# Filler matmuls dealt out 3-2-1 and 3-3-2 among three scans, and the opening's LoRA weights loaded ahead, in a two-layer diffusion trunk

## The chip, the cores and the metric

One core of one Trainium2 chip. The metric is device microseconds of one execution. Before the change three runs gave 3964.88, 3975.29 and 3981.9 us; their median, 3975.29 us, is the time before.

## What is computed

Two layers of one trunk over 256 context tokens (segment C) and 512 latent tokens (segment L), model width 1024, everything in float32. Each layer norms its input with shift and scale vectors that come from a conditioning vector (adaLN), projects it, and runs three mixers side by side: bidirectional RWKV-7 (8 heads of 64), bidirectional chunked gated DeltaNet (4 heads of 128) and grouped-query attention. The mixers' outputs are gated, merged and projected, then a SwiGLU follows. In the second layer the context is read but not written.

```
mod_x = (silu_c @ ada_w[l] + ada_b[l])[:, None, :]
sh1x, sc1x, g1x, sh2x, sc2x, g2x = jnp.split(mod_x, N_MOD, axis=-1)
hx = modulate(rmsnorm(x, norm1[l]), sh1x, sc1x)
px = jnp.split(hx @ lp['w_in'], IN_SPLIT_POINTS, axis=-1)
...
ya_x, _ = rwkv_branch(hx, px[0], lp, st_a)
yb_x, _ = gdn_branch(hx, px[1], px[2], lp, st_b)
yc_x = attn_latent(px[3], px[4], kc, vc, lp, cos, sin)
out_x = merge_branches(hx, ya_x, yb_x, yc_x, lp)
x = x + g1x * yx
x = x + g2x * swiglu(modulate(rmsnorm(x, norm2[l]), sh2x, sc2x), ffn_w1[l], ffn_w3[l], ffn_w2[l])
```

Both recurrences are computed in chunks of 64 tokens: inside a chunk with matmuls and the inverse of a small triangular matrix, from chunk to chunk with a state.

## The kernel before, in words

**Dense tiles.** A product of the whole input with 128 columns of a weight is a dense tile (`dense`, L251). Float32 accuracy comes from splitting each operand in a high and a low part, so each of the 8 blocks of the inner dimension takes three matmuls (`mm3`, L241 to L243): 24 matmuls of 512 columns for L (into `dL`) and 24 of 256 columns for C (into `dC`). The weight is loaded by SP into one of two buffers `wst` (L236), rounded by ACT to `whi` (L227), and the rest is formed by POOL as `wlo` (`split`, L231).

**Order.** Instructions are written in program order and a list scheduler puts them in order for each engine, by priority and by a simulated time; an engine then runs its instructions in that order. The priority is the place in the program, and `high_priority(offset)` moves a block ahead by so many instructions (HPG = 400 or 300 for DeltaNet, HPR = 700 for RWKV).

**The opening** (`build`, L280). The input segments `xC` and `xL` are loaded, squared (ACT, L386), summed (DVE, L388, `acc`), summed over partitions by a matmul (L390, `ssC`, `ssL`) and scaled. Four pieces of the adaLN vectors of layer 0 (`ada`, L338, pieces 0 to 3) are each 2 MB of weights in four loads (`adaw`, L345), 16 matmuls (`adaps`, L349, 8 in the program), an ACT copy (`adasb`, L351) and four small matmuls (`adamp`, L354); DVE adds the bias into `MOD` (L357). When all four are there, `norm1` writes the normed input in two parts, `hh` (ACT, L405) and `hl` (DVE or POOL, L407). Piece 0 is traced in the C turn of the loop, a first 96-column LoRA weight (`self.first`, `l1m`) in the L turn, pieces 1 to 3 after the loop.

**The first products** (`lora_g`, L757). They are the dense tile of `self.first`, then two of a 128-column LoRA weight (one with the shift mix, `l1m`, one without, `l1w`). In layer 0 that weight is loaded here; in layer 1 it was loaded in `norm1` and lies in `self.second`. From the first product come the DeltaNet decay rows (`brC`, `gcC`, `brL`, `gcL`), turned by small matmuls (`tsp`, L1205); from the last, the gate.

**The passes** (`layer`, L593). DeltaNet runs in 2 passes (p0, p1), RWKV in 4 (j0 to j3). A pass has three groups of four chunks, in the order C, L0, L1. A group has a preparation (for RWKV the matmuls `lps`, `aps`, `tps`, `tpv`; for DeltaNet `kkp`, `gtp`), the inverse of its eight triangular blocks (`inverse`, L878: DVE, ACT and POOL work with five rounds of 16 small matmuls `ips`, L931), and four steps, 0 to 3, each of which needs the state of the step before (RWKV: `Xp`, `Up`, `SP`, `Op`; DeltaNet: `KS`, `GU`, `GSO`). "L0 step 2" below is the stretch from the first `Xp` (or `KS`) of that step to the first of the next.

Between the groups the program places the pass's 8 units (dense tiles for the next pass or for the merge gates): after group number i it emits as many as a table says, DeltaNet by `GD`, RWKV by `RD`:

```
for grp, n in zip((("C", 0), ("L", 0), ("L", 1)), RD[j]):
    with tc.high_priority(offset=HPR[l]):
        self.r_group(j, *grp)
    self.fill(min(n, len(self.units) - keep))
self.flush(keep)
```

What is left is emitted after the three groups (`flush`), in DeltaNet and in RWKV's last pass with two units kept for the end.

Of the kernel before, what the change touches and what calls it, by code (L numbers as in the profile page):

```python
# [8 lines left out]
F32 = mybir.dt.float32  # L9
# [29 lines left out]
AD = (0, 1, 2, 3)  # L39
ORD = (1, 2, 3, 6, 5, 7, 4)  # L40
LOV = ((1,), (1, 3, 5))
GD = ((5, 4, 0), (5, 4, 0))
RD = ((4, 4, 0), (4, 4, 0), (4, 4, 0), (2, 2, 0))


PV = {}
# [157 lines left out]
class Prog:  # L204
# [75 lines left out]
    def build(self):  # L280
        nc, tc, A = self.nc, self.tc, self.A
        self.pend = {"L": [], "C": []}
        pool = lambda name, bufs=1, **k: tc.tile_pool(name=name, bufs=bufs, **k)
        with tc.block(name="whole", schedule_with_timeline_sim=True), pool("cst") as cst, pool("wp", 2) as wp, pool("pp", 2, space=bass.MemoryType.PSUM) as pp, \
                pool("dr", space=bass.MemoryType.DRAM) as dr, pool("hp") as hp, pool("sb", 2) as sb:
            self.cst, self.wp, self.pp, self.dr, self.hp, self.sb = cst, wp, pp, dr, hp, sb
            self.dC, self.dc = pp.tile([128, 2, TC], F32, name="dC", tag="dC", bufs=1), 0
            C = cst.tile([128, NCO], F32, name="C")
            nc.sync.dma_start(C, A["co"][:, 0:NCO])
            self.C = C  # L290
            self.scv = cst.tile([128, 8, 32], F32, name="scv")
            nc.sync.dma_start(self.scv, A["cv"])
            nc.scalar.activation(self.scv, self.scv, AF.Silu)
            self.xsrc = {"C": A["xT"][:, :, 0:TC], "L": A["xT"][:, :, TC:T]}
            self.vectors(0)
            with tc.tile_pool(name="nx", bufs=2, reuse_waits="tile") as nx:
                x = {}
                self.nb = 8
                self.segs = ["L", "C"]
                ss = self.sums()  # L300
                self.tables()
                for s, n in (("C", TC), ("L", TL)):
                    x[s] = nx.tile([128, KT, n], F32, name="x" + s, bufs=1)
                    nc.sync.dma_start(x[s], self.xsrc[s])
                    if s == "C":
                        self.ada(0, 0, nx, 8, bank=("dL", 2))
                    else:
                        self.first = self.split(self.lora(0, 384, 96, 2, nx)[:])
                    for k in range(KT):
                        self.squares(x[s][:, k, :], k, s, ss)  # L310
                    self.settle()
                    rs = sb.tile([128, TL + 4], F32, name="rs", tag="up", bufs=2)[:, :n]
                    self.rstd_from(rs, ss[s], 1.0 / D, self.co("cb", 0, 1))
                    for k in range(KT):
                        nc.vector.tensor_tensor(x[s][:, k, :], x[s][:, k, :], rs, ALU.mult)
                for i in range(1, 4):
                    self.ada(0, i, nx, 8, bank=("dL", 2))
                self.norm1(0, x, nx)
            for l in range(DEPTH):
                self.l, self.nb = l, SB[l]  # L320
                self.last = l == DEPTH - 1
                self.P, self.MOD = self.Ps[l], self.MODs[l]
                self.layer()
                if self.upto is not None and self.upto[0] == l:
                    break
# [9 lines left out]
        self.nc.sync.dma_start(self.Ps[l], self.A["pv"][l])  # L335
        self.MODs[l] = self.cst.tile([128, 48, 2], F32, name=f"MOD{l}")

    def ada(self, l, n, pool, bufs=4, share=False, tag="adaw", bank=("iv", 1)):  # L338

        nc, A = self.nc, self.A  # L340
        ps = self.pp.tile([128, 512], F32, name="adaps", tag=bank[0], bufs=bank[1])
        for q in range(4):
            w = (self.wp.tile([128, 2, 512], F32, name="adaw", tag="wst") if share and q % 2 else
                 pool.tile([128, 2, 512], F32, name="adaw", tag=tag, bufs=bufs))
            nc.sync.dma_start(w, A["ada"][l, n][:, 2 * q:2 * q + 2, :])  # L345
            for i in range(2):
                k = 2 * q + i
                g = k % 4
                nc.tensor.matmul(ps[32 * g:32 * g + 32, :], self.scv[:, k, :], w[:, i, :], start=(k < 4), stop=(k >= 4))  # L349
        sb = pool.tile([128, 512], F32, name="adasb", tag="adasb", bufs=1)  # L350
        nc.scalar.copy(sb, ps)  # L351
        mp = self.pp.tile([128, 4, 2], F32, name="adamp", tag=bank[0], bufs=bank[1])
        for m in range(4):
            nc.tensor.matmul(mp[:, m, :], sb[:, 128 * m:128 * m + 128], self.co("sel2"), start=True, stop=True)  # L354
        ob, _ = PV["ada_b"]
        b = self.Ps[l][:, ob + 4 * n:ob + 4 * n + 4].unsqueeze(2).to_broadcast([128, 4, 2])
        nc.vector.tensor_tensor(self.MODs[l][:, 4 * n:4 * n + 4, :], mp, b, ALU.add)  # L357
# [235 lines left out]
    def layer(self):  # L593
# [14 lines left out]
        with pool("sx") as self.sx:  # L608
# [10 lines left out]
            with pool("sg") as self.sc:  # L619
# [5 lines left out]
                for p in range(2):  # L625
# [5 lines left out]
                    self.g_begin(p)  # L631
                    for grp, n in zip((("C", 0), ("L", 0), ("L", 1)), GD[p]):
                        with tc.high_priority(offset=HPG[l]):
# [9 lines left out]
        with pool("sr") as self.sc:  # L643
# [17 lines left out]
            for j in range(4):  # L661
# [5 lines left out]
                keep = 2 if j == 3 else 0  # L667
                for grp, n in zip((("C", 0), ("L", 0), ("L", 1)), RD[j]):
                    with tc.high_priority(offset=HPR[l]):
# [87 lines left out]
    def lora_g(self):  # L757

        nc, A, l, sc = self.nc, self.A, self.l, self.sc
        self.GC, self.BR, self.rw, self.re, gh = {}, {}, {}, {}, {}  # L760
        if l:
            wq, wm = self.second
        else:
            wq, wm = self.lora(l, 256, 128, 2, sc)
            wm = self.split(wm[:])
        ps = self.dense(*self.first, self.h, self.S12)
        for s in self.S12:
            n = TL if s == "L" else TC
            self.gdn_rows(s, n, ps[s])
            if s not in self.segs:  # L770
                continue
            z = self.mixed(s, ps, self.shifted(ps[s], n, 1, 0.5, 32, 32), 32)
            nc.scalar.activation(z[0:32], z[0:32], AF.Tanh, scale=0.5)
            nc.vector.tensor_scalar(z[0:32], z[0:32], 0.5, 0.5, ALU.mult, ALU.add)

            g = sc.tile([128, n], F32R, name="ghx" + s, bufs=1)
            nc.scalar.copy(g[0:32], z[0:32])
            nc.vector.tensor_tensor(g[32:64], z[0:32], g[0:32].bitcast(F32), ALU.subtract)
            nc.scalar.copy(g[64:96], z[0:32])
            gh["x", s] = g  # L780
        psq, up = self.lora_dense(wq, wm, self.segs)
        for s in self.segs:
            n = TL if s == "L" else TC
            z = self.mixed(s, psq, up[s])
            nc.scalar.activation(z, z, AF.Tanh, scale=0.5)
            nc.vector.tensor_scalar(z, z, 0.5, 0.5, ALU.mult, ALU.add)
            g = sc.tile([128, n], F32R, name="ghg" + s, bufs=1)
            gl = sc.tile([128, n], F32R, name="glg" + s, bufs=1)
            nc.scalar.copy(g, z)
            nc.gpsimd.tensor_tensor(gl, z, g[:].bitcast(F32), ALU.subtract)  # L790
            gh["g", s] = (g, gl)
        for j in range(4):
            g2 = self.g2_weights(j)
            for s in self.segs:
                n = TL if s == "L" else TC
                ps = self.psd(s)
                self.mm3(ps, g2[0], g2[1], *gh["g", s], True, False)
                nc.tensor.matmul(ps, g2[2], gh["x", s][0:96], start=False, stop=True)
                z = self.zt("gj", n)
                nc.scalar.copy(z, ps)  # L800
                t0 = TC if s == "L" else 0
                nc.gpsimd.dma_start(self.gd[:, j, t0:t0 + n], z)
# [931 lines left out]
```

## Time and profile before

| | |
|---|---|
| median of 3 runs | 3975.29 us (3964.88 to 3981.9) |
| profiled execution, its own time | 3986.69 us |
| its span, first to last instruction | 3984.9 us |
| mean granted TensorE clock | 0.906 |
| busy: PE, PEld, DVE, ACT, POOL | 90%, 73%, 61%, 42%, 37% of the span |
| loaded and stored | 296.61 MB, mean 74 GB/s |

PE is the matmul stream of TensorE and PEld its weight loads, which run beside it. The granted clock is 1.0 or 0.5 at any moment, of 2.4 GHz; a mean between them says how much of a stretch was at half. The profiled execution was 11.4 us longer than the median.

In time, from the trace: the opening to 47 us, the LoRA products to 113 us, attention of layer 0 to 335 us, DeltaNet to about 812 us, RWKV to about 1480 us, merge and SwiGLU to 2220 us, then the same for layer 1: DeltaNet from about 2465, RWKV from about 2850 to 3460 us, and its tail to the end.

### The profile page before, as it was taken

What the parts mean: (1) busy time and instruction counts of PE and PEld (TensorE: products, weight loads), DVE (VectorE), ACT (ScalarE), POOL (GpSimd) and SP (SyncE); (2) the same over time, 40 slices, a digit from 0 to 9 for tenths busy, and PEclk for the clock granted to TensorE, in tenths of its full rate; (3) what the DMA queues carried; (4) which work ended last, traced back from release to release, by engine and by line L of the source; (5) the groups of instructions that cost most, each with busy time, mean ns of one, the idle gap of its engine ahead of it and who ended that gap; (6) DMA issues with size and microseconds to landing.
All of it is one profiled execution on the core that took longest, in us unless ns stands there. A gap on an engine that the chain in (4) does not pass through costs nothing. (4 is left out here: it accounts for less than half of the span.)

```text
span 3984.9 us, 69791 instructions
## 1 busy us (share of the span) xinstructions
PE 3572.3 (90%) x27704; PEld 2928.8 (73%) x27704; DVE 2426.7 (61%) x4776; ACT 1681.5 (42%) x3207; POOL 1465.1 (37%) x1738
## 2 busy tenths in 40 slices
PE   7987878999899989899999798889998999898998
PEld 4655667777777768789999656666777777677887
DVE  5386745326766746565555557965167786467776
ACT  5455534334444432333333646543343443234334
POOL 3223213244233315454444424414241333164554
PEclk7998878999799999999999899989796988699999
DMA  5501111111011126422222251102120111252232
GB/s 190 172 30 51 32 33 50 53 57 55 13 53 38 40 71 199 153 80 69 70 69 59 94 179 53 51 25 75 39 63 9 53 32 47 96 186 66 93 96 82
DMA packets 121174, 296.61 MB, mean 74 GB/s; under 512 B 15024, under 2 KB 41824, under 8 KB 120464
## 3 DMA queue, kind: packets, MB, share of 16 engines
q1 hardware_dynamic: 111408, 260.16, 20.9%
q0 software_dynamic: 9440, 31.99, 2.1%
q8 instruction: 218, 3.57, 0.4%
q14 instruction: 108, 0.88, 0.1%
HBM read 257.87 MB, written 34.23 MB: 73 GB/s over the span
## 5 line engine op out<-in xcount | busy, mean ns | idle before, releaser
L231 POOL TENSOR_TENSOR wlo<-wst,whi 128x512 fp32r<-128x512 f32 (+3 forms) x606 | 693.0, 1164 | 784.1 <-ACT whi L227 755.4
L227 ACT CAST whi<-wst 128x1024 fp32r<-128x1024 f32 (+3 forms) x303 | 266.0, 878 | 512.3 <-PE dC L243 193.4
L241 PE MATMUL dL<-hh,whi 128*128 128x512 f32 x1040 | 436.3, 420 | 21.3 <-ACT tg L710 4.5
L242 PE MATMUL dL<-hl,whi 128*128 128x512 f32 x1040 | 423.7, 407 | 3.7 <-DVE hl L407 2.3
L243 PE MATMUL dL<-hh,wlo 128*128 128x512 f32 x1040 | 422.8, 407 | 0.1
L241 PEld LDWEIGHTS dL<-hh,whi 128*128 128x128 f32 x1040 | 202.1, 194 | 79.6 <-issue 6.9
L242 PEld LDWEIGHTS dL<-hl,whi 128*128 128x128 f32 x1040 | 201.9, 194 | 51.5 <-issue 7.5
L241 PE MATMUL dC<-hh,whi 128*128 128x256 f32 x704 | 220.7, 313 | 18.4 <-ACT ct L371 9.3
L243 PEld LDWEIGHTS dL<-hh,wlo 128*128 128x128 f32 x1040 | 201.3, 194 | 48.3 <-issue 2.5
L242 PE MATMUL dC<-hl,whi 128*128 128x256 f32 x704 | 213.2, 303 | 4.8 <-DVE hl L407 2.4
L243 PE MATMUL dC<-hh,wlo 128*128 128x256 f32 x704 | 212.2, 301 | 0.0
L502 POOL TENSOR_TENSOR sl<-S,sh 128x512 fp32r<-128x512 f32 x110 | 152.7, 1392 | 154.8 <-ACT sh L501 115.4
L241 PE MATMUL q<-g2h,sh 128*128 128x384 f32 (+1 forms) x528 | 166.8, 318 | 16.3 <-DVE c L524 13.8
L241 PEld LDWEIGHTS dC<-hh,whi 128*128 128x128 f32 x704 | 144.9, 206 | 35.3 <-ACT ct L371 11.9
L242 PE MATMUL q<-g2l,sh 128*128 128x384 f32 (+1 forms) x528 | 166.6, 316 | 2.9 <-DVE g2l L447 2.9
L243 PE MATMUL q<-g2h,sl 128*128 128x384 f32 (+1 forms) x528 | 165.1, 314 | 0.0
L242 PEld LDWEIGHTS dC<-hl,whi 128*128 128x128 f32 x704 | 145.2, 206 | 13.0 <-issue 3.9
L501 ACT CAST sh<-S 128x512 fp32r<-128x512 f32 x176 | 105.0, 619 | 105.0 <-PE q L242 63.7
L243 PEld LDWEIGHTS dC<-hh,wlo 128*128 128x128 f32 x704 | 145.1, 206 | 3.2 <-issue 1.7
L524 DVE TENSOR_TENSOR c<-c,q 128x384 f32<-128x384 f32 (+1 forms) x220 | 106.0, 482 | 61.7 <-PE q L243 50.6
L241 PE MATMUL dL<-fh,whi 128*128 128x512 f32 x352 | 138.3, 393 | 3.0 <-ACT fh L578 1.6
L242 PE MATMUL dL<-fl,whi 128*128 128x512 f32 x352 | 138.1, 392 | 0.0
(545 smaller groups left out, 10008.8 us busy)
## 6 DMA issues: line engine op xcount, KB each, us to landing
adaw<-in_ada SPq DMA_DIRECT2D x96, 512.0 KB
wst<-in_win SPq DMA_DIRECT2D x68, 512.0 KB
wst<-in_wg SPq DMA_DIRECT2D x48, 512.0 KB
w<-in_f SPq DMA_DIRECT2D x45, 512.0 KB
wst<-in_f SPq DMA_DIRECT2D x43, 512.0 KB
t<-tg POOLq DMA_DIRECT2D x48, 256.0 KB, 2.6
tgL<-t SPq DMA_DIRECT2D x48, 256.0 KB
wst<-in_f SPq DMA_DIRECT2D x48, 256.0 KB
```

Of the source, the lines that this page charges most:

```text
L227: nc.scalar.copy(hi, wt)
L231: nc.gpsimd.tensor_tensor(lo[:, a:b], wt[:, a:b], hi[:, a:b].bitcast(F32), ALU.subtract)
L241: nc.tensor.matmul(ps, wh, xh, start=first, stop=False)
L242: nc.tensor.matmul(ps, wh, xl, start=False, stop=False)
L243: nc.tensor.matmul(ps, wl, xh, start=False, stop=last)
L501: nc.scalar.copy(hi, src)
L502: (nc.vector if i in LOV[l] else nc.gpsimd).tensor_tensor(lo, src, hi[:].bitcast(F32), ALU.subtract)
L524: add = lambda d, a, b: nc.vector.tensor_tensor(d, a, b, ALU.add)
```

## The change

1. The tables. In `layer`, after the groups C, L0 and L1 a pass emitted 5, 1 and 0 of its units (DeltaNet; the table's 4 met what was left) or 4, 4 and 0 (RWKV), and now emits 3, 2, 1 or 3, 3, 2; RWKV's last pass 2, 1, 1 in place of 2, 2, 0. In DeltaNet two units stay for the end, as before.
2. The opening. `ada` has 12 buffers for its weights in place of 8, and its small matmuls write to another bank of PSUM than the large ones. Pieces 1 to 3 are traced ahead of the L segment's squares, not after the loop.
3. The 128-column LoRA weight of layer 0 is loaded and its mixed part split in the opening, ahead of `norm1`; `lora_g` finds it in `self.second`.

```diff
-GD = ((5, 4, 0), (5, 4, 0))
-RD = ((4, 4, 0), (4, 4, 0), (4, 4, 0), (2, 2, 0))
+GD = ((3, 2, 1), (3, 2, 1))
+RD = ((3, 3, 2), (3, 3, 2), (3, 3, 2), (2, 1, 1))
...
                     if s == "C":
-                        self.ada(0, 0, nx, 8, bank=("dL", 2))
+                        self.ada(0, 0, nx, 12, bank=("dL", 2), mbank=("ch", 2))
                     else:
+
+                        for i in range(1, 4):
+                            self.ada(0, i, nx, 12, bank=("dL", 2), mbank=("ch", 2))
                         self.first = self.split(self.lora(0, 384, 96, 2, nx)[:])
...
-                for i in range(1, 4):
-                    self.ada(0, i, nx, 8, bank=("dL", 2))
+                wq, wm = self.lora(0, 256, 128, 2)
+                self.second = wq, self.split(wm[:])
                 self.norm1(0, x, nx)
...
-        mp = self.pp.tile([128, 4, 2], F32, name="adamp", tag=bank[0], bufs=bank[1])
+        mbank = mbank or bank
+        mp = self.pp.tile([128, 4, 2], F32, name="adamp", tag=mbank[0], bufs=mbank[1])
...
-        if l:
-            wq, wm = self.second
-        else:
-            wq, wm = self.lora(l, 256, 128, 2, sc)
-            wm = self.split(wm[:])
+        wq, wm = self.second
```

What the scheduler makes of it, at three places.

**The opening, on PE and SP.** PE before, from its first matmul to the first dense one:

```order
L349 MATMUL adaps<-adaw,scv 32x512 x4
L390 MATMUL ssC<-acc,C 128x256
L349 MATMUL adaps<-adaw,scv 32x512 x4
L354 MATMUL adamp<-C,adasb 128x2 x4
L349 MATMUL adaps<-adaw,scv 32x512 x6
L390 MATMUL ssL<-acc,C 128x512
L349 MATMUL adaps<-adaw,scv 32x512 x2
L354 MATMUL adamp<-C,adasb 128x2 x4
L349 MATMUL adaps<-adaw,scv 32x512 x8
```

The same place now, PE's row with `ssL` and the two around it:

```order
L352 MATMUL adaps<-adaw,scv 32x512 x8
L394 MATMUL ssL<-acc,C 128x512
L358 MATMUL adamp<-C,adasb 128x2 x4
L352 MATMUL adaps<-adaw,scv 32x512 x8
L358 MATMUL adamp<-C,adasb 128x2 x4
```

The last two matmul pairs of piece 1 stood behind `ssL` and now stand ahead of it. SP's loads before, from `xL` on:

```order
L304 DMA xL<-in_xT 128x8x512
L729 DMA l1w<-in_l 128x8x96
L345 DMA adaw<-in_ada 128x1024 x4
L236 DMA wst<-in_win 128x1024 x2
L335 DMA P_15142<-in_pv 128x233
L345 DMA adaw<-in_ada 128x1024 x8
L729 DMA l1w<-in_l 128x8x128
```

SP now:

```order
L304 DMA xL<-in_xT 128x8x512
L348 DMA adaw<-in_ada 128x1024 x8
L733 DMA l1w<-in_l 128x8x96
L733 DMA l1w<-in_l 128x8x128
L338 DMA P_15142<-in_pv 128x233
L348 DMA adaw<-in_ada 128x1024 x4
L236 DMA wst<-in_win 128x1024
```

Two projection weights that stood ahead of pieces 2 and 3 now come behind the last piece; the 128-column LoRA weight that stood behind it comes ahead. On DVE the three instructions that mix the 96-column weight (L737 to L739) stood among the seven `acc` additions of segment L and now follow them all, and so does the split on POOL.

**The end of the first LoRA product, on PE** (`dL_390` is the first product's L part, `dL_505` the second's). Before:

```order
L242 MATMUL dL_390<-hl_276,whi_158 128x512
L243 MATMUL dL_390<-hh_275,wlo_159 128x512
L1205 MATMUL tsp_734<-C_74,gcC_430 64x8 x2
L1205 MATMUL tsp_734<-C_74,brC_415 64x8 x2
L1205 MATMUL tsp_734<-C_74,gcC_430 64x8 x2
L1205 MATMUL tsp_734<-C_74,brC_415 64x8 x2
L1205 MATMUL tsp_734<-C_74,gcC_430 64x8 x2
L1205 MATMUL tsp_734<-C_74,brC_415 64x8 x2
L241 MATMUL dL_505<-hh_275,whi_361 128x512
```

Now:

```order
L241 MATMUL dL_390<-hh_285,whi_233 128x512
L243 MATMUL dL_505<-hh_285,wlo_279 128x512
L242 MATMUL dL_390<-hl_286,whi_233 128x512
L243 MATMUL dL_390<-hh_285,wlo_234 128x512
L241 MATMUL dL_390<-hh_285,whi_233 128x512
L242 MATMUL dL_390<-hl_286,whi_233 128x512
L243 MATMUL dL_390<-hh_285,wlo_234 128x512
L241 MATMUL dL_505<-hh_285,whi_278 128x512
```

The `tsp` matmuls, which wait for `gcC`, stood between the two products and now stand behind both parts of the second; the four `adaps` matmuls of piece 4 that stood among them stand later too.

**Layer 1, RWKV pass j1, steps L0 2 and L0 3, on PE.** Before, the end of L0 step 3:

```order
L242 MATMUL dC<-hl,whi 128x256
L243 MATMUL dC<-hh,wlo 128x256
L1074 MATMUL Up<-Xs,TT 64x64 x4
L1081 MATMUL SP<-UV,BT 64x64 x4
L1090 MATMUL Op<-INC,UV 64x64 x4
L1093 MATMUL Op<-AR,S 64x64 x4
L1059 MATMUL Xp<-UV,LK 64x64 x4
L1062 MATMUL Xp<-S,AR 64x64 x4
L1025 MATMUL aps<-AR,BK 128x64 x8
```

Now, L0 step 2 and the start of L0 step 3:

```order
L243 MATMUL dC<-hh,wlo 128x256
L931 MATMUL ips<-TT,Y_29229 64x32 x16
L1059 MATMUL Xp<-UV,LK 64x64 x4
L1062 MATMUL Xp<-S,AR 64x64 x4
L1074 MATMUL Up<-Xs,TT 64x64 x4
L1081 MATMUL SP<-UV,BT 64x64 x4
L1090 MATMUL Op<-INC,UV 64x64 x4
L1093 MATMUL Op<-AR,S 64x64 x4
L1059 MATMUL Xp<-UV,LK 64x64 x4
L1062 MATMUL Xp<-S,AR 64x64 x4
```

The last dense matmul of the pass stood in L0 step 3 and now stands ahead of L0 step 2: the steps from L0 2 on have none.

## Rows read from the trace of the kernel before

**Rows 1.** Busy time by stage: window, length, PE, PEld, DVE, ACT, POOL, clock, DMA, GB/s

```profile
0.00:47.00 47.00, 25.91 (x100) 8.86 (x100) 20.41 (x52) 16.34 (x32) 3.38 (x10) 0.78 0.80 300
47.00:115.00 68.00, 59.32 (x358) 43.74 (x359) 33.61 (x57) 41.89 (x79) 31.89 (x42) 0.82 0.39 125
...
335.00:812.00 477.00, 393.62 (x3223) 319.77 (x3222) 265.17 (x532) 210.15 (x398) 130.34 (x200) 0.84 0.16 46
812.00:1480.00 668.00, 608.70 (x6612) 495.37 (x6611) 396.85 (x1001) 273.62 (x570) 219.81 (x336) 0.92 0.13 40
...
2465.00:2850.00 385.00, 329.17 (x2780) 260.49 (x2781) 239.29 (x477) 177.55 (x337) 118.74 (x173) 0.85 0.15 44
2850.00:3460.00 610.00, 557.94 (x5772) 443.55 (x5771) 388.93 (x934) 246.77 (x513) 185.11 (x283) 0.84 0.14 43
```

**Rows 2.** Timeline of PE, the opening: start us, us, engine, line, operation

```profile
29.07 1.30 PE L390 MATMUL ssL<-acc,C 128*128 128x512 f32 x2 [2.37 <-DVE acc L388]
...
40.90 3.21 PE L349 MATMUL adaps<-adaw,scv 128*32 128x512 f32 x16
...
47.03 0.58 PE L241 MATMUL dC<-hh,whi 128*128 128x256 f32 x1 [1.10 <-ACT hh L405]
```

**Rows 3.** Timeline of DVE, the opening

```profile
21.09 1.49 DVE L388 TENSOR_TENSOR acc<-acc,sq 128x512 f32<-128x512 f32 x2 [2.34 <-ACT sq L386]
22.49 0.42 DVE L737 TENSOR_TENSOR l1m<-l1w,P 128x256 f32<-128x256 f32 x1
...
24.10 4.91 DVE L388 TENSOR_TENSOR acc<-acc,sq 128x512 f32<-128x512 f32 x4
```

**Rows 4.** Timeline of POOL, the opening

```profile
25.53 2.93 POOL L231 TENSOR_TENSOR wlo<-l1m,whi 128x512 fp32r<-128x512 f32 x2 [25.09 <-ACT whi L227]
```

**Rows 5.** DMA view of 0 to 60 us: GB/s in 40 slices of 1.5 us; issues

```profile
GB/s 0 172 369 327 377 326 399 393 410 406 392 384 351 396 412 404 412 410 388 407 418 399 410 407 410 216 0 0 11 0 0 0 0 5 42 319 32 0 0 0
...
wst<-in_win SPq DMA_DIRECT2D x2, 512.0 KB
...
l1w<-in_l SPq DMA_DIRECT2D x1, 512.0 KB
```

**Rows 6.** Timeline of PE, the LoRA products

```profile
64.32 0.39 PE L242 MATMUL dL<-hl,whi 128*128 128x512 f32 x1
64.55 0.39 PE L243 MATMUL dL<-hh,wlo 128*128 128x512 f32 x1
68.63 0.39 PE L1205 MATMUL tsp<-C,gcC 40*64 40x8 f32 x4 [3.70 <-DVE gcC L1176]
...
75.42 0.63 PE L243 MATMUL dL<-hh,wlo 128*128 128x512 f32 x1
75.85 0.63 PE L241 MATMUL dL<-hh,whi 128*128 128x512 f32 x1
```

**Rows 7.** Timeline of ACT, the LoRA products

```profile
84.55 0.38 ACT L720 ACTIVATE up<-dC 128x256 f32<-128x256 f32 x1
89.92 0.63 ACT L785 ACTIVATE z<-z 128x512 f32<-128x512 f32 x1 [4.99 <-DVE z L747]
```

**Rows 8.** Busy time in stretches of the passes, columns as in rows 1

```profile
996.70:1068.60 71.90, 60.18 (x834) 50.06 (x832) 53.67 (x144) 24.17 (x64) 14.25 (x29) 0.69 0.03 9
...
1172.70:1249.60 76.90, 65.35 (x797) 52.07 (x794) 60.56 (x156) 33.02 (x69) 22.76 (x40) 0.89 0.06 17
...
3162.40:3177.70 15.30, 14.80 (x224) 12.48 (x221) 3.02 (x10) 4.80 (x15) 4.67 (x6) 1.00 0.31 88
3177.70:3215.90 38.20, 33.61 (x456) 27.56 (x456) 29.15 (x82) 11.69 (x32) 6.48 (x19) 0.69 0.01 2
```

**Rows 9.** The same view, steps without dense matmuls

```profile
768.50:784.20 15.70, 10.91 (x120) 8.66 (x121) 4.87 (x17) 4.39 (x14) 0.00 (x0) 1.00 0.00 1
...
2798.00:2829.00 31.00, 24.93 (x160) 20.63 (x160) 6.19 (x22) 6.97 (x23) 0.00 (x0) 0.50 0.02 5
...
3420.60:3433.40 12.80, 10.49 (x152) 8.95 (x151) 3.86 (x16) 2.58 (x11) 0.00 (x0) 0.50 0.00 1
```

More of the change, by code (lines that the diff above doesn't have):

```diff
@@ L336, in vectors, with ada @@
         self.MODs[l] = self.cst.tile([128, 48, 2], F32, name=f"MOD{l}")
-    def ada(self, l, n, pool, bufs=4, share=False, tag="adaw", bank=("iv", 1)):
+    def ada(self, l, n, pool, bufs=4, share=False, tag="adaw", bank=("iv", 1), mbank=None):
         nc, A = self.nc, self.A
```

## Prediction, written before the changed kernel ran

> **What bounds the kernel now.** I read the busy time by stage first [rows 1]. In the passes PE is the bound, but not evenly: in RWKV of layer 0 it is busy 608.7 of 668 us, in DeltaNet of layer 0 only 393.6 of 477, and in both layers the clock is well under 1 (0.84 to 0.92). DVE, ACT and POOL are busy 64% or less there. So a pass holds stretches where PE is full, and stretches where a chain of waits through several engines sets the pace; the next view separates them. In the opening, the DMA share of 0.80 says that loads set the pace; in the LoRA products PE has gaps (59.3 of 68 us) at a clock of 0.82.
>
> Then I cut a pass into steps by the first `Xp` or `KS` of each. Steps that hold dense matmuls are full: the two steps L0 2 and L0 3 of layer 1's j1 take 15.3 us with PE busy 14.8 at full clock, and the five after them, which have none, take 38.2 us with PE busy 33.6 at clock 0.69 [rows 8]. Steps without anything but the chain show what the clock does: three in DeltaNet take 15.7 us at clock 1.00 (5.2 each), four in layer 1 take 31.0 us at 0.50 (7.75 each), and three in RWKV 12.8 us at 0.50 (4.3 each) [rows 9]. The first three ran just after a dense stretch, the others after longer ones without dense work.
>
> Last I read the timelines of the opening and the LoRA products. The first dense matmul starts at 47.03 us [rows 2], the first product ends at 64.9, then PE waits 3.70 us for the decay rows and comes back at half clock: dense starts 0.43 us apart (75.42, 75.85) against 0.23 (64.32, 64.55) at full clock [rows 6].
>
> **The change, part by part.**
>
> *The opening: 5 us less.* PE's matmul `ssL` waited for the last `acc` addition and started at 29.07, and everything of pieces 2 and 3 stood behind it [rows 2]. The seven additions should take 7 x 0.7 us from 21.09; the first two took 1.49 together [rows 3]. But three mixing instructions of 0.42 stood among them, and the last four took 4.91, while POOL's split ran (25.53, 2.93 us) [rows 3, 4]. Both are gone from there, so the additions end at 21.1 + 4.9 = 26.0, 3 us sooner, and piece 1 no longer splits around `ssL`. Then the loads bind. They ran at about 405 GB/s until the slice from 37.5, which is half full, so to about 38.3 us; two loads of 512 KB leave, one comes in [rows 5]: 0.52 MB less, 1.3 us, so the last piece lands at 37.0. From there a quarter of the last 16 matmuls (0.8 of 3.21) and the tail that ran from their end, 44.1, to the first dense matmul at 47.0 (2.9) [rows 2] give 40.7. I allow 1.3 for the landing that has to be seen and for PE and ACT waking one after the other, and take 42.0: 5 us less. The bounds: 3 (only `ssL` moves, and the pieces still follow one another on PE), and 6.3.
>
> *The LoRA products: another 5 us less.* PE now goes from the first product straight into the second, with the `tsp` matmuls behind both. From 64.9 the second product and the L part of the third are 48 `dL` matmuls at 0.23 and 24 `dC` at half that, 14 us; ACT's row says when they were done, since it waited 4.99 us for DVE, which waited for PE, and started at 89.92 [rows 7]. So about 89.2 - 64.9 - 14 = 10 us went to the wait, the half clock and the small matmuls. Not all of it comes back, because ACT is next in line: it had its own work done at 84.9 [rows 7]. That work is nearly the same now and starts 5 us sooner, so ACT is free at 79.9, and the matmuls are done by 60 + 14 + 1 = 75. The ACT row then starts at 79.9, not 89.92: 10 us for the opening and the products together. From 113 us on, attention is mostly PE's own work, so I carry it over whole. For both I take -10, from -15 (ACT's decay chain starts sooner too) to -3 (the pieces 4 to 6 and projection weights, now issued later, hold attention up).
>
> *The tables in layer 0: 4 us less; in layer 1: nothing.* The change does not do what its numbers say. Units are low in priority but ready, so PE takes them as soon as a group leaves a hole, wherever they stand. Counted in PE's order, each pass has the same dense matmuls as before, and they run out sooner, not later: in layer 1, j1 the last one stands ahead of step L0 2, where it stood in L0 3. The moved dense work, at 0.23 and 0.12 us each, is in layer 0 4.7 us in j0, 8.8 in j1, 2.5 in j2; in layer 1 7.5 in p1, 8.0 in j1, 5.1 in j2: 36.6 us. In p0 of both layers, in j3 and in j0 of layer 1 next to nothing moves. In a full step dense work costs its own time wherever it stands, so a move is free if the step that it leaves gets shorter by as much. Layer 1, j1: the two steps lose 8.0 of their 15.3 us [rows 8] and keep 7.3, and two bare steps at half clock take 8.6 [rows 9]; against that the steps ahead have a few microseconds of idle PE to fill. That is zero, and the other two like it. In layer 0 the order also brings the next groups' inverses together: in j0 the five rounds for L1 stood on both sides of the start of L1, and now all stand ahead; from j1 to j2 the rounds for C stood half in the next pass's dense stretch, and now stand in the bare steps. The two stretches have 71.9 - 60.2 = 11.7 and 76.9 - 65.4 = 11.5 us of idle PE [rows 8]. I take a sixth of these 23 us, 4. The bounds come below as rivals: all six passes lose their bare idle, or all the moved work is added.
>
> *Costs set to nothing.* The 12 buffers and the other bank cost no instruction. The two projection weights issued later are attention's, which PE reaches at about 113 us, and next to nothing is loaded from 39 to 49 us [rows 5]. If that cover failed, attention would start late, and the -3 above holds it.
>
> **Sum.** -10 - 4 = -14. The profiled execution took 3986.7 and should come to 3972.7; it was 11.4 over the median, so the median goes from 3975.3 to 3961.
>
> **The rivals.** *The passes gain for real.* If the dense work that ends sooner frees DVE and POOL for preparation and inverse, the bare stretches lose their idle time: 38.2 - 33.6 = 4.6 us in the one of layer 1 [rows 8], in six passes 28 in place of 4. With the opening: 3975 - 10 - 28 = 3937. For it speaks that DVE is busy 29 of these 38 us, so the bare stretch hangs on it; against it, that its work is the same. The Trainium skill, in Trace Analysis, Identifying the Most-Contended Engine, says that matmul busy time misjudges TensorE and that weight-load busy time is the measure of headroom. By that rule the passes have more to give than PE's 91% says, as PEld is busy 495 of 668 us [rows 1], and this case would be the likeliest; but the full steps above, where PE never waits, bear it out for the bare ones only.
>
> *The opening's gain is spent.* If attention waits for its own loads or for ACT and not for PE, 10 becomes 0, and 3971 is left.
>
> *Slower: the bare stretches take no shorter time.* If the steps which lose their dense work are held by the inverse rather than by PE, they keep their length, and the 36.6 us are added to steps that are full already: 3975 - 10 + 37 = 4002. It decides where a step that loses work has rounds of an inverse in it; for it speaks that the half clock makes such steps longer still, 7.75 against 5.2 us [rows 9]; against it, that L0 2 and L0 3 in layer 1 get their rounds ahead of them in the new order. In the Trainium skill, TensorE: Matmul & The Clock Gate, Part 1, half clock is the resting state and activity lifts it; the rows agree, and by it alone a longer bare stretch means more half clock, though only some 1 us a step in RWKV's.
>
> **How the numbers follow.** The forecast, 3953 to 3969 by itself, has 0.48; the real gain in the passes 0.22; the spent gain 0.20; slower 0.10. A measurement of this kernel can tell 0.5% from no change, 20 us: under 3955 or over 3995. Faster is the second case and a quarter of the first, 0.34; slower 0.10; the same 0.56. The range reaches from the second case's 3937, with 3 to spare, to 3984, which is the opening's gain with half of the moved work added; it leaves out the slower rival's price and the tails.
>
> **What would show it.** First dense matmul at 42 (over 44: the loads or `ssL` still bind). No PE wait for `gcC`, and ACT's row at 80 (89.9 before). Layer 1, j1: steps L0 2 and L0 3 together 7 to 9 us, and a clock under 0.69 in the stretch after. If those two still take 12 or more, the slower rival holds. If the windows of layer 0's passes lose 10 us or more each, the first rival does. I would be wrong altogether if layer 1's stages, where only the tables act, moved by more than 10 us.

## The result, and the profile after

The changed kernel took 4020.28 us (median of 8 runs, 3994.84 to 4030.78) against 3975.52 us before (8 runs, 3964.88 to 3998.32): a ratio of 1.0108, 95% interval 1.009 to 1.0127. It is 1.1% slower, where 14 us less were forecast, and outside the range. The profiled execution took 4030.78 us with a span of 4029.0 us and a mean clock of 0.894 (before 3986.69, 3984.9 and 0.906). Both profiled executions lie some 11 us over their medians, so their difference, 44 us, is the one to be explained.

Busy time by stage, profile of the changed kernel (window, length, PE, PEld, DVE, ACT, POOL, clock, DMA share, GB/s), to be held against [rows 1]:

```profile
0.00:43.50 43.50, 23.69 (x101) 7.67 (x101) 21.61 (x55) 18.11 (x34) 6.07 (x13) 0.87 0.87 314
43.50:111.00 67.50, 61.52 (x358) 47.30 (x359) 29.65 (x54) 40.42 (x76) 27.97 (x40) 0.78 0.38 132
...
331.00:810.00 479.00, 404.45 (x3199) 328.48 (x3200) 262.82 (x524) 198.99 (x387) 127.80 (x197) 0.83 0.14 43
810.00:1526.00 716.00, 656.84 (x6635) 534.20 (x6633) 407.24 (x1002) 277.44 (x576) 219.86 (x338) 0.85 0.12 39
...
2511.00:2895.00 384.00, 329.10 (x2788) 262.52 (x2789) 243.94 (x479) 178.99 (x338) 120.45 (x176) 0.85 0.15 45
2895.00:3506.00 611.00, 554.80 (x5763) 443.46 (x5762) 386.39 (x934) 245.13 (x511) 180.36 (x279) 0.84 0.14 42
```

Most of the loss is in one stage. RWKV of layer 0 takes 716 us in place of 668; in layer 1 DeltaNet and RWKV together take 949.8 us against 945.3, and the opening ends sooner. In that one stage PE has the same work (6635 records against 6612) and is busy 48 us longer, while DVE, ACT and POOL do much what they did. The clock says why: 0.85 in place of 0.92.

The cut from the first `Xp` of j0 to that of the last step of j3 is the same work. Before, and then after, where the stretches that answer to [rows 8] follow:

```profile
912.00:1459.10 547.10, 501.40 (x5989) 406.55 (x5988) 357.21 (x911) 228.99 (x502) 168.52 (x254) 0.92 0.12 39
```

```profile
916.50:1501.10 584.60, 539.32 (x5987) 438.54 (x5989) 364.41 (x908) 227.91 (x500) 166.38 (x251) 0.84 0.12 36
...
1001.10:1082.00 80.90, 67.69 (x826) 55.33 (x825) 56.99 (x147) 23.16 (x63) 15.22 (x30) 0.60 0.03 8
1189.50:1269.30 79.80, 71.86 (x737) 57.41 (x739) 62.64 (x151) 30.53 (x69) 21.01 (x37) 0.70 0.06 16
...
3221.50:3228.30 6.80, 5.01 (x111) 3.92 (x107) 2.42 (x9) 2.04 (x8) 0.14 (x2) 1.00 0.04 13
3228.30:3266.30 38.00, 33.55 (x454) 27.54 (x454) 29.05 (x82) 11.52 (x32) 6.28 (x19) 0.69 0.01 2
```

37.5 us longer, of which PE is busy 37.9 longer; its idle time is the same, 45.7 and 45.3 us. The two stretches around the ends of j0 and j1 have 21.1 us of idle PE together in place of 23.2 [rows 8], but their clock went from 0.69 to 0.60 and from 0.89 to 0.70. Counted over the records of this cut, 835 chain matmuls start at half clock in place of 384, 238 of the preparation in place of 63, 542 of the inverse in place of 364, and 50 dense ones in place of 26. The groups by line show it as a mean: before, then after (line, operation, shapes, count | busy us, mean ns | idle before):

```profile
L241 PE MATMUL dL<-hh,whi 128*128 128x512 f32 x184 | 77.2, 419 | 0.0
...
L1025 PE MATMUL aps<-AR,BK 64*128 64x128 f32 x352 | 39.0, 303 | 2.6 <-DVE INC L1033 1.3 <-DVE AR L1002 1.1
...
L1059 PE MATMUL Xp<-UV,LK 64*64 64x64 f32 x376 | 23.1, 244 | 2.7 <-DVE S L1083 2.4
```

```profile
L241 PE MATMUL dL<-hh,whi 128*128 128x512 f32 x184 | 80.5, 438 | 0.6 <-ACT osq L375 0.6
...
L1025 PE MATMUL aps<-AR,BK 64*128 64x128 f32 x352 | 45.6, 351 | 6.5 <-DVE AR L1002 4.7 <-DVE INC L1033 1.8
...
L1059 PE MATMUL Xp<-UV,LK 64*64 64x64 f32 x376 | 29.3, 266 | 6.6 <-DVE S L1083 4.6 <-ACT o L1098 1.7
```

The counts are equal, the dense matmuls take 5% longer, the `aps` of the preparation 16%, the chain's `Xp` 9%.

DeltaNet of layer 0 adds some 10 us (554.5 us from the first `KS` to the first `Xp` of j0, 544.2 before), also with PE busy longer (485.1 against 468.6), though a second profile of the kernel before will show how much of that is chance.

The opening did what was forecast. Timeline of PE, changed kernel:

```profile
26.32 1.13 PE L394 MATMUL ssL<-acc,C 128*128 128x512 f32 x2 [0.32 <-DVE acc L392]
...
35.03 4.80 PE L352 MATMUL adaps<-adaw,scv 128*32 128x512 f32 x16 [2.39 <-DMA adaw<-in_ada]
...
42.80 0.58 PE L241 MATMUL dC<-hh,whi 128*128 128x256 f32 x1 [1.17 <-ACT hh L409]
...
66.91 0.28 PE L1205 MATMUL tsp<-C,gcC 40*64 40x8 f32 x4
...
69.30 0.54 PE L241 MATMUL dL<-hh,whi 128*128 128x512 f32 x1 [1.75 <-ACT up L724]
```

The additions on DVE ahead of `ssL`, and ACT's row of [rows 7]:

```profile
20.80 5.47 DVE L392 TENSOR_TENSOR acc<-acc,sq 128x512 f32<-128x512 f32 x7 [2.26 <-ACT sq L390]
...
79.80 0.63 ACT L785 ACTIVATE z<-z 128x512 f32<-128x512 f32 x1 [1.39 <-DVE z L751]
```

But attention, whose first matmul on PE is `pn`, began at 125.7 us against 129.6, 4 us sooner and not 10, and DeltaNet 5.8 us sooner. Before, then after:

```profile
129.59 0.68 PE L1449 MATMUL pn<-aq,C 128*128 128x256 f32 x2
```

```profile
125.70 0.70 PE L1449 MATMUL pn<-aq,C 128*128 128x256 f32 x2
```

The 40 us ahead of attention, before and after:

```profile
90.00:130.00 40.00, 40.00 (x289) 28.80 (x288) 3.96 (x13) 14.88 (x32) 15.41 (x18) 0.96 0.51 168
```

```profile
86.00:126.00 40.00, 40.00 (x231) 27.77 (x230) 2.07 (x10) 10.13 (x24) 8.88 (x15) 0.82 0.54 178
```

PE is busy without a gap in both; it has its own work there, and now does it at a lower clock.

### The profile page after: what moved, and what is told of

The parts are those of the page before. It is cut to its first block, busy times and chain, and to the rows that moved or that the text cites. A ratio compares the mean times of both kernels' runs of the same rounds, so it can differ in the third digit from the quotient of the medians.

```text
span 4029.0 us, 69776 instructions
## 1 busy us (share of the span) xinstructions
PE 3625.2 (90%) x27704; PEld 2975.9 (74%) x27704; DVE 2431.8 (60%) x4776; ACT 1675.1 (42%) x3203; POOL 1458.7 (36%) x1738
```

## Experiments

Two measures recur. **Half clock** is the time that an execution spent at the lower level, 2 x (1 - mean clock) x span, as a median over its timed executions. **Stage** is the length of layer 0's RWKV, from the first `Xp` of j0 to that of j3's last step, in the profiled execution. Before, after and the runs with "same work" have the same instructions in the passes, which differ in order alone. The kernel before took 3971 to 3975 us beside each of these runs.

| run | what differs from the kernel before | median us | ratio (95%) | half clock | stage |
|---|---|---|---|---|---|
| before | nothing | 3975.52 | 1 | 699 | 547.1 |
| after | all of the change | 4020.28 | 1.0108 (1.009 to 1.0127) | 852 | 584.6 |
| before_again | nothing | 3976.3 (one) | | 707 | 547.1 |
| e1_opening | opening and LoRA, same work | 3987.55 | 1.0036 (1.0021 to 1.005) | 749 | 559.0 |
| e2_tables | both tables, same work | 3998.52 | 1.0067 (1.0043 to 1.009) | 767 | 565.9 |
| e3_rd | RWKV's table, same work | 4017.63 | 1.0111 (1.0088 to 1.0133) | 791 | 574.2 |
| e4_gd | DeltaNet's table, same work | 4001.93 | 1.0065 (1.0048 to 1.0083) | 768 | 560.5 |
| o_order | pieces traced ahead, same work | 3971.12 | 0.9988 (0.9972 to 1.0005) | 687 | 546.7 |
| o_buffers | 12 buffers, same work | 3994.35 | 1.0039 (1.0023 to 1.0055) | 778 | 550.3 |
| o_rest | opening without the 12 buffers, same work | 3982.5 | 1.0016 (0.9996 to 1.0036) | 756 | 556.7 |
| rd_layer1 | RWKV's table in layer 1, same work | 3974.79 | 1.0 (0.9985 to 1.0014) | 699 | 547.3 |
| rd_layer0 | RWKV's table in layer 0, same work | 4010.68 | 1.0091 (1.007 to 1.0112) | 787 | 572.5 |
| rd431 | 4, 3, 1 in layer 0, same work | 4024.25 | 1.012 (1.0096 to 1.0145) | 804 | 572.1 |
| rd800 | 8, 0, 0 in layer 0, same work | 4004.35 | 1.0072 (1.0048 to 1.0097) | 768 | 578.2 |
| w1_wide | after, with 296 wide matmuls | 4059.95 | 1.0223 (1.0183 to 1.0263) | 710 | 578.8 |
| w2_narrow | after, with 296 narrow ones | 4105.04 | 1.0323 (1.028 to 1.0366) | 907 | 599.4 |
| w3_before_wide | before, with 296 wide ones | 4035.58 | 1.0162 (1.0114 to 1.0211) | 710 | |
| h1_hold2 | two units held back | 4020.55 | 1.0114 (1.0098 to 1.013) | 731 | 562.7 |
| h2_hold3 | three units held back | 4049.06 | 1.0188 (1.016 to 1.0217) | 846 | |
| h3_after_hold2 | after, with two held back | 4015.99 | 1.0112 (1.0089 to 1.0134) | 775 | |

**The parts of the change.** `e1_opening` is the changed kernel with the tables of before; the other three are the kernel before with one or both new tables.

```diff
-GD = ((5, 4, 0), (5, 4, 0))
+GD = ((3, 2, 1), (3, 2, 1))
-RD = ((4, 4, 0), (4, 4, 0), (4, 4, 0), (2, 2, 0))
+RD = ((3, 3, 2), (3, 3, 2), (3, 3, 2), (2, 1, 1))
```

> Only the opening and LoRA part of the change, with the tables of before. Theory A (the new RWKV table costs the time, by clock: in layer 0's RWKV the trace of the changed kernel has 204 us at half clock in place of 102, with the same matmuls and the same idle time of PE): the opening's gain is left alone, about 6 us, since DeltaNet of layer 0 started 5.8 us earlier in the changed kernel: 3966 to 3972 us beside 3975.5 of before, and RWKV of layer 0 at its clock of 0.92. Theory B (any shift of the opening makes the scheduler sort the passes anew, and the tables are not to blame): over 3995 us, with the clock of that stage near 0.85. Theory C (DeltaNet's table costs it, and RWKV's only passes it on): as A.

> Only the two tables, with the opening of before. Theory A: the loss without the opening's gain, 45 + 6 = 51 us over before, 4026 us, and RWKV of layer 0 near a clock of 0.85. Theory B: within 10 us of before, 3966 to 3986. Theory C: as A.

> Only RWKV's table, with the opening and DeltaNet's table of before. Theory A: most of the loss, about 40 us (what passes j0 to j3 of layer 0 lost between the two traces), 4015 us; layer 1 unchanged within 10 us. Theory C: under 3985. Theory B: within 10 us of before.

> Only DeltaNet's table, with the opening and RWKV's table of before. Theory A: up to 10 us slower, 3975 to 3986 (pass p1 of layer 0 lost about 10 us in the changed kernel's trace). Theory C: 4015 or more. Theory B: within 10 us of before.

No theory stands as it was put. RWKV's table alone costs as much as the whole change (1.0111), as A says. But the opening alone costs too, and so does DeltaNet's table, and the parts do not add: 0.65% and 1.11% give 0.67% together. A loss that is the sum of moved work would add. What does go along with the time in all of them is the half clock.

**Is it the clock?** Each execution's clock is on record. Over 179 timed executions of before, after and the kernels with the same work, span and half clock lie on one line, 3738 us + 0.33 us per us at half clock (correlation 0.93). Within one kernel, where the order is fixed, the line is less steep: 0.27 over 72 executions of the kernel before (correlation 0.87), and 0.27 when each of the 13 kernels is taken about its own mean. So the 0.33 may hold waits of the new orders besides the clock. For the changed kernel, 153 us more at half clock are 41 us at 0.27, of 45 lost. To move the clock itself, I added matmuls that nothing needs to the steps without dense work, wide ones and, as a control, the same number of narrow ones:

```diff
+    def warm(self, U, n, lo, w):
+        x = self.h["L"][0]
+        for _ in range(n):
+            self.nc.tensor.matmul(U[:, lo:lo + w], x[:, 0, 0:128], x[:, 0, 0:w], start=True, stop=True)
...
+            if l in (0, 1) and (final or (seg == "C" and st == 0 and j > 0)):
+                self.warm(UU, 4, 128, 384)
...
+            if l in (0, 1) and (final or (seg == "L" and p == 0)):
+                self.warm(UU, 6, 256, 256)
```

> The changed kernel with work added that nothing needs: 296 wide matmuls on PE in the steps that have no dense matmuls (RWKV: 4 of 384 columns behind each Up in group L1 and in the first C step of j1 to j3; DeltaNet: 6 of 256 columns behind each GU in L0 and L1 of p0 and L1 of p1). At the 0.23 us that 512 columns take at full clock they are 43 us of PE's time, part of it in its waits. Theory clock (the loss is preparation, inverse and chain running at half clock because PE does too little in the bare steps): time at half clock falls from 852 us by 150 or more, and with 0.34 us per us of it (the slope over the 55 timed executions so far) the kernel is no slower than 4020 in spite of the added work, and near 3990 if half of that work falls into waits. Theory order (the loss is the order itself: waits and steps in a row that take as long at any clock): time at half clock may fall, but the time is 4020 to 4063 us.

> The same 296 added matmuls in the same places with 16 columns each: as many instructions, hardly any work. Theory clock: half clock stays within 60 us of 852, and the time within 20 us of 4020. Theory order: the same. If this one falls as far as the wide one, it is the new order that the added instructions bring, and not the clock.

> The kernel before with the same 296 wide matmuls. Theory clock: time at half clock falls from 699 us (median of its 17 timed executions) by 100 or more, and the time is under 3975, about 3955 if half of the added work falls into waits. Theory order: 3975 to 4018 us.

Layer 0's RWKV in the profile with the wide ones, and with the narrow ones:

```profile
918.20:1497.00 578.80, 532.96 (x6059) 431.62 (x6059) 361.95 (x910) 227.88 (x502) 167.13 (x254) 0.91 0.11 36
```

```profile
949.80:1549.20 599.40, 553.63 (x6057) 453.70 (x6059) 363.20 (x910) 228.99 (x502) 165.81 (x254) 0.84 0.11 35
```

The numbers expected were missed: 296 matmuls cost 85 us even with 16 columns each, which I had put at next to nothing. Nothing needs what they compute, but they write to the tile of `Up` or `GU`, and ACT's copies of these tiles wait for them. From the view of the line that adds them (L1108) in the narrow run: who waited for it, us and times.

```profile
  ACT UV L1078: 87.0, 32
  ACT GUs L1391: 77.9, 22
```

So both runs lengthen the chain itself. Against each other, with 16 to 24 times the columns, the wide kernel is 45 us faster (intervals 1.0183 to 1.0263 and 1.028 to 1.0366), has 197 us less at half clock, and runs the stage at 0.91 in place of 0.84 with the same idle time of PE (45.8 us). But the two also differ in order: by their traces, some 2700 of PE's 28000 matmul records stand elsewhere. So the pair shows again that time goes with the clock; that the wider work is what lifted it, and not the other order, is not shown. On the kernel before, whose clock in that stage was 0.92 already, the wide ones lift nothing (710 us) and only cost.

**Does a second profile of the kernel before agree?**

> The kernel before once more, for a second profile of the same program: the profiled execution shown ahead of the prediction had 752 us at half clock, its timed ones a median of 699. Theory clock: this one's time lies on the line 3734 + 0.34 us per us at half clock within 15 us, whatever it is; the stages that differ from the first profile are those whose half clock differs. Theory order: the two profiles differ in waits, not in clock.

It does: the line gives 3738 + 0.33 x 707 = 3971 us of span, measured were 3974.5. RWKV of layer 0 took 547.1 us in both profiles; what differs is DeltaNet of layer 0, 544.2 against 538.1 us with the same work, at a clock of 0.87 and 0.89. Six us between two profiles are thus chance in DeltaNet, and not in layer 0's RWKV. In eight profiles with the old order there, DeltaNet of layer 0 takes 535.4 to 545.8 us; the changed kernel's 554.5 lies 9 above them.

**Would really spread dense work help?** The tables do not hold a unit back, since PE takes it as soon as it is ready. Here the weight's load is made to wait:

```diff
-    def load_w(self, src, kt=KT):
+    def load_w(self, src, kt=KT, after=None):
         wt = self.wp.tile([128, kt, 128], F32, name="wst", tag="wst")
+        if after is not None:
+            self.nc.gpsimd.tensor_copy(wt[:, 0, 0:1], after)
...
+                    if grp == ("L", 0):
+                        for u, c in zip(held, (128, 192)):
+                            u(after=self.R[j]["o", "L"][:, c:c + 1])
```

> The kernel before, with the last two units (gates) of RWKV passes j0, j1 and j2 really held back: POOL copies one element of the pass's output into the weight's buffer ahead of its load, so that the load waits for step L0 2 (first unit) and L0 3 (second). In the program two dense tiles then stand among the steps of L1, which were bare, and the full steps have two fewer. Theory clock: the bare stretches get shorter, the time at half clock falls from about 699 us by 60 or more, and at 0.34 us for each the kernel takes 3950 or less. Theory order (the passes are paced by the chain and the inverse, whatever PE's clock): within 10 us of before, 3962 to 3982, or slower where POOL's queue waits behind the held copy.

> The changed kernel with the same two units held back in j0 to j2. Theory clock: layer 0's RWKV, at 204 us of half clock in the changed kernel, comes down to 120 or less, and the time from 4020 to 3985 or less. Theory order: 4010 to 4030.

> The kernel before with three units held back in j0 to j2 (behind steps L0 1, L0 2 and L0 3). Theory clock: at least as good as with two where the full steps still hold enough dense work; half clock 640 us or less, 3955 or less. If now the steps of group C and L0 lose their clock instead, half clock moves there and the time is back near 3972.

Held back in this way it does not, and here the clock is not the main reason. Pass j1 of layer 1, before and with two held:

```profile
3078.50:3210.30 131.80, 123.73 (x1394) 96.85 (x1392) 95.41 (x234) 58.53 (x124) 42.45 (x66) 0.90 0.13 40
```

```profile
3097.90:3241.40 143.50, 123.28 (x1404) 97.35 (x1398) 93.51 (x233) 58.89 (x124) 43.04 (x67) 0.87 0.12 37
```

PE is busy as long as before and the pass is 11.7 us longer: PE is idle 20.2 us in place of 8.1. Of these 12 us, 4.9 stand in step L0 1, which lost its dense work, and 4 in L0 3, in a wait for a held weight itself, whose rounding on ACT waited for its load. The step and the wait:

```profile
3165.60:3173.70 8.10, 3.23 (x49) 2.51 (x48) 8.05 (x17) 3.90 (x10) 0.93 (x2) 0.77 0.00 0
```

```profile
3189.69 0.80 PE L243 MATMUL dL<-hh,whi 128*128 128x512 f32 x1 [4.51 <-ACT whi L227]
```

So the hold brings a wait of its own, and the three runs do not show what spread work would do without one. In this run half clock rose by 32 us, 11 us by the line, of 46 lost. The theory's number for the changed kernel (3985 or less) fell as well: 4016.

**Why does the opening cost?** Its pieces apart. `o_order` traces the adaLN pieces ahead, and leaves every engine's order as it was from attention on. `o_buffers` changes one number and moves 4056 of PE's 20588 instructions, nearly all in the passes. `o_rest` is the opening's part without that number.

```diff
-                        self.ada(0, 0, nx, 8, bank=("dL", 2))
+                        self.ada(0, 0, nx, 12, bank=("dL", 2))
...
-                    self.ada(0, i, nx, 8, bank=("dL", 2))
+                    self.ada(0, i, nx, 12, bank=("dL", 2))
```

> Of the change only this: pieces 1 to 3 of the adaLN vectors are traced ahead of the L segment's squares. The instructions of each engine are then in the order of before from attention on, to the last one; in the opening ssL follows all of piece 1. Theory start (the passes pay because they begin at another moment): slower than before by 5 us or more. Theory order of the scheduler (the passes pay because they are sorted anew): 0 to 5 us faster than before, 3967 to 3974, with the passes at the clock of before.

> Of the change only the 12 buffers for the adaLN weights in place of 8. The passes' work is the same, but the scheduler's simulated times shift and 4056 of PE's 20588 instructions stand elsewhere in its order, nearly all in the passes. Theory start: the opening hardly moves, so within 5 us of before. Theory order of the scheduler: slower by 5 to 15 us, like the opening's part as a whole (14), with more time at half clock in the passes.

> The opening's part without the 12 buffers: pieces traced ahead, small matmuls in another bank, and the 128-column LoRA weight loaded ahead. 3604 of PE's instructions stand elsewhere. Theory start: slower by about 14 us, like the whole part. Theory order of the scheduler: slower by 0 to 15; the passes decide, and most of the 6 us at DeltaNet's start is there all the same.

This fits the order of the passes as the cause. With it untouched the piece is 0.12% faster, which the interval does not quite tell from nothing; with 12 buffers, which add no instruction anywhere, the kernel is 0.39% slower. Layer 0's RWKV in the profiles of `o_order` and then of `o_buffers`:

```profile
905.00:1451.70 546.70, 499.05 (x5987) 404.37 (x5987) 357.12 (x910) 229.16 (x502) 168.55 (x254) 0.92 0.12 39
```

```profile
914.60:1464.90 550.30, 502.90 (x5984) 409.34 (x5984) 365.80 (x908) 227.16 (x500) 165.06 (x251) 0.90 0.12 38
```

In `o_order` DeltaNet began 4.6 us sooner (363.3 against 367.8 and 368.0 us), and this stage is as long as before, so the start itself costs nothing. In `o_buffers` the loss is not in this stage alone: it takes 3 us more, and DeltaNet began at 374.1 us, 6 later than before. Where the rest of its 0.39% goes is not settled by one profile.

**Which layer, and what in the order?** `rd_layer1` and `rd_layer0` use the new table in one layer; `rd431` and `rd800` put other numbers in layer 0's:

```diff
+R0 = ((4, 3, 1), (4, 3, 1), (4, 3, 1), (2, 2, 0))
...
-                for grp, n in zip((("C", 0), ("L", 0), ("L", 1)), RD[j]):
+                for grp, n in zip((("C", 0), ("L", 0), ("L", 1)), (RD if l else R0)[j]):
```

> RWKV's new table in layer 1 alone, with everything else as before. The theory that the table costs where it adds preparation and inverse to bare steps (layer 0; in layer 1 these stood in bare steps before): within 8 us of before, 3964 to 3980. The rival that the table costs about the same in both layers: 3985 or more, since it cost 46 us in the two together.

> RWKV's new table in layer 0 alone, all else as before. With rd_layer1 at 0, theory clock in layer 0: all of the 46 us of the run with RWKV's table, 4010 to 4022. The rival that both layers must change together: under 3990.

> Layer 0's RWKV passes with 4, 3 and 1 units behind C, L0 and L1, all else as before: it moves a unit towards the end, but in PE's order the dense matmuls of the next pass still begin in C step 0 of j2 and j3, with 80 to 96 inverse matmuls beside them. Theory start of the dense work: within 12 us of before, 3963 to 3987, with j2 of layer 0 near its 15 us at half clock. The rival that units moved to the end cost by their number: about a third of the 46, 3988 or more.

> Layer 0's RWKV passes with all 8 units behind C (4 in j3), all else as before: the other direction, nothing is held towards the end; but in PE's order the dense matmuls of the next pass begin a step later in j2 and j3, as in the changed kernel, and the inverse of the next group stands alone. Theory start of the dense work: slower by 20 us or more, 3995 to 4020, with 35 us or more at half clock in j2. The rival that it is the direction that counts: no slower than before.

The table is free in layer 1 (1.0000) and costs in layer 0 (1.0091). The rest of my reading fell. I had seen that in the changed kernel the next pass's dense matmuls begin a step later, so that an inverse and a preparation stand alone, and took that to be the fault; but the table 4, 3, 1 begins them as before and is among the slowest. The direction isn't it either, as 8, 0, 0 costs too. Layer 0's RWKV with 4, 3, 1, and with 8, 0, 0:

```profile
905.50:1477.60 572.10, 518.29 (x5987) 418.80 (x5988) 356.38 (x910) 229.25 (x502) 168.53 (x254) 0.89 0.12 37
```

```profile
910.90:1489.10 578.20, 521.37 (x5987) 423.16 (x5987) 367.31 (x910) 229.86 (x502) 166.25 (x254) 0.88 0.12 36
```

Of 25 and 31 us, PE's longer busy time is 17 and 20, and 8 and 11 are idle. All ten other orders of these passes that were run, with the same work, take 550 to 585 us here, and the four profiles in the old order 546.7 to 547.3. So the old order is a good one, by clock and by waits, and none of the new ones is. What makes it good remains open: neither the start of the dense work nor the number or direction of the moved units tells it. That it was picked from many such orders would explain it, but no run shows that.

## Why the prediction was wrong

*The opening, -5: right in the mechanism, a little large.* `ssL` went from 29.07 to 26.32 behind additions that end at 20.80 + 5.47 = 26.27 (26.0 forecast), and the first dense matmul came at 42.80 (42.0). Some of the 4.2 us against [rows 2] is chance: over the twelve profiles with the old opening that matmul came between 44.1 and 47.8 us, over the five with the new one between 42.8 and 43.7, with medians 3.4 us apart.

*The LoRA products, -5 more: the row was hit, in part by luck, and the gain was not carried.* The wait for `gcC` is gone and ACT's row came at 79.80 (79.9 forecast). But ACT had its own work done at 78.41 and waited 1.39 us for DVE, where the forecast had ACT's own work set the time; and PE then waited 1.75 us for ACT's `up` and came back at half clock all the same (dense starts 0.43 us apart from 70.05 on). The step "so I carry it over whole" failed. From the first dense matmul to attention it is 82.9 us, 82.6 before, so nothing of this 5 us arrived there: between that row and attention PE has 40 us of work without a gap, whose length no wait decides, and did it at 0.82 instead of 0.96. With 4 us at attention and 5.8 at DeltaNet the two came out near the small end of the -15 to -3 given.

*The tables in layer 1, nothing: right.* L0 2 and L0 3 took 6.8 us together (7 to 9 forecast), the stretch behind them 38.0 at 0.69 (38.2 at 0.69 before; I had expected a lower clock), DeltaNet took 446.1 us against 449.4 and RWKV 503.7 against 495.9, and RWKV's table in that layer alone measured 1.0000. With that the slower rival fell too: it wanted steps that keep their length when they lose dense work. The direction it named came, by another road. The first rival fell as well, as it wanted 10 us or more off layer 0's passes.

*The tables in layer 0, -4: the step that failed.* It counted idle PE, 23 us in two stretches, and took a sixth of it as gain; the idle time hardly changed, and the stage got 37.5 us longer with PE busy. I had the price of a longer bare stretch in hand, 5.2 against 7.75 us a step [rows 9], and put it at "only some 1 us a step in RWKV's". But the chain is not all that stands there: preparation and inverse do as well. The prediction saw that inverse rounds "now stand in the bare steps", and gave them no price at half clock. Besides 451 more matmuls of the chain, 175 more of the preparation and 178 of the inverse began at half clock. Half clock in this cut went from 92 to 189 us, and 97 us at 0.33 is 32 of the 37.5 (26 at the 0.27 of one kernel).

*What no rival held.* All of them priced the moves that the change intends. DeltaNet's table alone costs three fifths of the loss, RWKV's all of it, and the opening, which touches no pass, a third, because the scheduler sorts everything behind a change anew. The ten new orders of layer 0's passes came out 0.2 to 1.2% slower, nine of them clear of noise; a rival "the new order as such, wherever it comes from" was missing, though [rows 9] show that a change of clock in the same steps has a price.

## What to carry to other kernels

Where a scheduler orders the program, compare the order of every engine far behind the edit, and split the edit into what leaves that order alone and what doesn't; only the first can be priced from rows. Idle PE is half of the matter in a stretch of small matmuls: ask also what its clock will be, and price a microsecond at half clock by the kernel's own executions (here 0.27 us; 0.33 across the orders), from their spans and clocks. When matmuls are added as a probe, look at who waits for them, and compare the orders of the probe and its control. Two profiles of the same program differed by 6 us in one stage, so a small term wants runs and not a profile.

## What the runs showed of the hardware

I had not expected a kernel of one core to spend 699 of 3973 us at half clock, nor that its executions scatter along one line with it. The Trainium skill, TensorE: Matmul & The Clock Gate, section HAM oscillation — how this bites in real kernels, takes half of the throttled time as the loss; here 0.33 us per us was measured over 13 kernels and 0.27 within one, and the measurement decides. And added matmuls of 16 columns are not free where a copy in the chain waits for them: 296 of them cost 85 us, 0.29 us each, some of which may be due to the new order that they bring and to 55 us more at half clock.
